# A two-layer decoder trunk on one core: low parts in pieces of 256 columns on GpSimd, and the delta net's convolution shared differently between VectorE and ScalarE

## The chip, the cores and the metric

The kernel runs on one core of a Trainium2 chip. A core has TensorE (PE in the profile; PEld is its loading of weights), VectorE (DVE), ScalarE (ACT), GpSimd (POOL) and SyncE (SP, which issues DMAs here). The engines run at the same time, each through its own list of instructions in order, and wait for each other by semaphores. Data lie in SBUF (128 partitions) and products land in PSUM (banks of 128 x 512 f32). The metric is the device time of one execution in microseconds (us).

## The reference

Two layers over 1024 tokens of width 1024. Layer 0 mixes tokens by RWKV-7, layer 1 by a gated DeltaNet; each is followed by a dense SwiGLU part, with layer norms and a modulation from a conditioning vector. The change touches two things: the split of f32 operands into a high and a low part, which the kernel uses for every dense product, and the delta net's projections with their causal convolution of four taps:

```python
def _gated_deltanet_mixer(u, w_in, conv_w, a_log, dt_bias, norm_g, w_out):
    ...
    proj = u @ w_in
    qkv = jax.nn.silu(_causal_depthwise_conv(proj[..., :3 * hd], conv_w))
    z = proj[..., 3 * hd:4 * hd].reshape(B, T, H, d)
    ...
    q = _l2norm(qkv[..., :hd].reshape(B, T, H, d)) * d ** -0.5
    k = _l2norm(qkv[..., hd:2 * hd].reshape(B, T, H, d))
    v = qkv[..., 2 * hd:].reshape(B, T, H, d)
    ...
    o = _chunk_gated_delta_rule(q, k, v, g, beta)
    o = _rms_norm(o, norm_g, 1e-6) * jax.nn.silu(z.astype(F32))
    return o.reshape(B, T, hd).astype(u.dtype) @ w_out
```

## The kernel before

The tokens are handled in two halves of 512 columns; channels lie on partitions, eight groups of 128. Every dense product is made of three: weight high times activation high, weight high times activation low, weight low times activation high (`mm3`, L258 to L263). A high part is a copy in a reduced f32 form, a low part the difference of the source and its high part (`split`, L220 to L225; the difference is recorded as L212, the line of the helper `tt`). One weight is 128 x 1024 (all eight groups of input channels for 128 outputs), so one output tile takes 24 matmuls of 512 columns.

`weight` (L238) brings one weight: a DMA into `wr` (2 buffers), the high part `wh` by ACT, the low part `wl` by POOL unless the caller names DVE (3 buffers each). A low part that is needed again for the second half of the tokens is stored to memory by SP (L236) and read back there instead of being computed a second time. So POOL makes low parts mostly while the first half of a layer's weights passes: for the RWKV projections, the first dense half of layer 0 (about 700 to 1400 us, woven with the RWKV units), the delta net's projections for the first half of the tokens (1500 to 1720 us) and the first dense half of layer 1 (2460 to 2820 us, woven with the delta net's heads).

`proj_gdn(h, kinds)` (L1264) makes the delta net's projections of half `h`, tile by tile. `kinds` (1, 0) are k and q, eight tiles each, in the function `turn` (L1486); `kinds` (4,) are v and z in turns, woven with the heads and the dense part. A tile of k, q or v goes this way: eight times three matmuls into a PSUM bank `mm`; ACT copies the bank to `x` (L1289, columns 3 to 514); DVE puts zeros ahead of it and saves the last three columns in `ctail` for the second half (L1292, L1293), or takes them from `ctail` (L1295); DVE makes the last tap (L1296, a multiplication by a number per partition) and adds the other three (L1298, recorded as L215); ACT takes tanh (L1303), DVE makes silu from it (L1304, recorded as L215), SP stores the tile. For k and q ACT squares it into `th` (L1307), and the next call of `flush` hands the squares to PE, which sums them over the partitions into the bank `rows` (`sums`, L338). `flush` stood behind the next tile's matmuls. After the eighth tile of a kind `rows_out` turns the sums into factors on DVE.

The pieces are Python generators. `interleave` (L971) and `weave` (L775) draw from several of them by costs written at each `yield`; so the code of a projection tile is issued among that of layer norms, gates or heads. The framework then sets each engine's list from this, may move an instruction ahead of or behind others where its operands allow it (the sums of squares stand in the middle of a later tile's matmuls), and adds the waits. Tiles come from pools with a fixed number of buffers for each name: `e` has 5 (here `x`, the tile and `th` of each projection), `rows` 2 banks and `mm` 6 banks in `turn`.

## Time and profile before

| | |
|---|---|
| median of 3 runs | 3426.49 us (3426.42 to 3430.7) |
| the profiled execution | 3418.32 us |
| its span, first to last instruction | 3416.5 us |
| TensorE's mean granted clock | 0.970 |
| PE, PEld busy | 3229.8, 2464.8 us |
| DVE, ACT, POOL busy | 2207.9, 1374.5, 974.0 us |

The span is read by stages, since the engines that PE waits for differ between them. Idle time of an engine that nobody waits for costs nothing; what counts here are PE's waits, and in front of them the DVE operation or the ACT operation that ended late. A duration in the timeline runs from the start of an instruction to its end and holds whatever the instruction waits for once it has been issued.

### The profile page before, as it was taken

What the parts mean: (1) busy time and instruction counts of PE and PEld (TensorE: products, weight loads), DVE (VectorE), ACT (ScalarE), POOL (GpSimd) and SP (SyncE); (2) the same over time, 40 slices, a digit from 0 to 9 for tenths busy, and PEclk for the clock granted to TensorE, in tenths of its full rate; (3) what the DMA queues carried; (4) which work ended last, traced back from release to release, by engine and by line L of the source; (5) the groups of instructions that cost most, each with busy time, mean ns of one, the idle gap of its engine ahead of it and who ended that gap; (6) DMA issues with size and microseconds to landing.
All of it is one profiled execution on the core that took longest, in us unless ns stands there. A gap on an engine that the chain in (4) does not pass through costs nothing. (4 is left out here: it accounts for less than half of the span.)

```text
span 3416.5 us, 51830 instructions
## 1 busy us (share of the span) xinstructions
PE 3229.8 (95%) x19408; PEld 2464.8 (72%) x19408; DVE 2207.9 (65%) x4630; ACT 1374.5 (40%) x2622; POOL 974.0 (29%) x725
## 2 busy tenths in 40 slices
PE   7989999988999999988999999999989999999997
PEld 3667777765666676766777777777767778878886
DVE  5667888877666666587676555586577763573235
ACT  4656777634333333344332222345323223342222
POOL 2443233343333333443321000220133333420001
PEclk8999999997999999999999999999999999999998
DMA  7872334352444444644664554556644446565543
GB/s 260 274 242 89 114 106 132 122 171 82 159 148 165 145 165 141 217 165 175 223 209 166 182 170 168 199 187 218 223 166 157 151 151 235 182 209 185 197 174 135
DMA packets 240524, 594.12 MB, mean 174 GB/s; under 512 B 24720, under 2 KB 80656, under 8 KB 240272
## 3 DMA queue, kind: packets, MB, share of 16 engines
q1 hardware_dynamic: 240128, 590.74, 51.1%
q8 instruction: 152, 2.49, 0.3%
q14 instruction: 100, 0.82, 0.1%
q10 hardware_dynamic: 144, 0.07, 0.0%
HBM read 440.04 MB, written 150.67 MB: 173 GB/s over the span
## 5 line engine op out<-in xcount | busy, mean ns | idle before, releaser
L261 PE MATMUL mm<-s,wh 128*128 128x512 f32 x2608 | 1081.3, 415 | 14.0 <-DVE s L224 5.9
L262 PE MATMUL mm<-s,wh 128*128 128x512 f32 x2608 | 1057.9, 406 | 14.6 <-DVE s L212 8.2
L263 PE MATMUL mm<-s,wl 128*128 128x512 f32 x2608 | 1050.0, 403 | 0.0
L212 POOL TENSOR_TENSOR wl<-wr,wh 128x1024 fp32r<-128x1024 f32 (+1 forms) x243 | 504.4, 2082 | 981.9 <-ACT wh L222 912.4
L261 PEld LDWEIGHTS mm<-s,wh 128*128 128x128 f32 x2608 | 497.4, 191 | 129.2 <-issue 19.8
L262 PEld LDWEIGHTS mm<-s,wh 128*128 128x128 f32 x2608 | 498.4, 191 | 112.3 <-DVE s L212 12.7
L263 PEld LDWEIGHTS mm<-s,wl 128*128 128x128 f32 x2608 | 497.5, 191 | 95.1 <-issue 1.2
L249 ACT CAST wh<-wr 128x1024 fp32r<-128x1024 f32 x199 | 206.6, 1049 | 500.4 <-PE mm L262 260.3
L222 ACT CAST wh<-wr 128x1024 fp32r<-128x1024 f32 (+1 forms) x254 | 228.2, 905 | 343.9 <-PE mm L262 201.1
L215 DVE SCALAR_TENSOR_TENSOR x<-mm,modp,x 128x512 f32<-128x512 f32 x272 | 202.1, 747 | 73.9 <-PE mm L263 72.0
L261 PE MATMUL mm<-ys,wh 128*128 128x512 f32 x544 | 219.6, 404 | 2.9 <-DVE x L215 2.8
L262 PE MATMUL mm<-ys,wh 128*128 128x512 f32 x544 | 217.3, 400 | 0.0
L263 PE MATMUL mm<-ys,wl 128*128 128x512 f32 x544 | 217.3, 399 | 0.0
L212 DVE TENSOR_TENSOR e<-mm,e 128x512 f32<-128x512 f32 x88 | 60.6, 689 | 168.7 <-PE mm L263 168.4
L212 DVE TENSOR_TENSOR s<-e,s 128x512 fp32r<-128x512 f32 x106 | 122.2, 1154 | 60.8 <-ACT s L222 60.6
L833 PEld LDWEIGHTS <-z 128*128 128x128 f16 x1600 | 83.8, 98 | 103.3 <-issue 64.2
L215 DVE SCALAR_TENSOR_TENSOR e<-e,mm 128x512 f32<-128x512 f32 x88 | 60.2, 684 | 141.8 <-ACT e L676 141.4
L215 DVE SCALAR_TENSOR_TENSOR tx<-mm,modp,tx 128x512 f32<-128x512 f32 x112 | 83.1, 748 | 79.4 <-PE mm L263 79.1
L261 PEld LDWEIGHTS mm<-ys,wh 128*128 128x128 f32 x544 | 103.7, 191 | 29.7 <-DVE x L215 3.7
L263 PEld LDWEIGHTS mm<-ys,wl 128*128 128x128 f32 x544 | 103.5, 190 | 25.7
L262 PEld LDWEIGHTS mm<-ys,wh 128*128 128x128 f32 x544 | 103.7, 191 | 25.2 <-issue 0.5
L215 DVE SCALAR_TENSOR_TENSOR e<-e,vec,e 128x512 f32<-128x512 f32 x144 | 115.0, 799 | 3.8
(389 smaller groups left out, 5418.8 us busy)
## 6 DMA issues: line engine op xcount, KB each, us to landing
wr<-w_in SPq DMA_DIRECT2D x176, 512.0 KB, 4.5
ada<-ada_w SPq DMA_DIRECT2D x96, 512.0 KB, 4.8
loi<-wl SPq DMA_DIRECT2D x88, 512.0 KB, 3.0
wr<-w_ffo SPq DMA_DIRECT2D x88, 512.0 KB, 4.9
wl<-loi SPq DMA_DIRECT2D x88, 512.0 KB, 3.6
wr<-w_g SPq DMA_DIRECT2D x64, 512.0 KB, 4.5
lof<-wl SPq DMA_DIRECT2D x44, 512.0 KB, 2.9
wl<-lof SPq DMA_DIRECT2D x44, 512.0 KB, 3.5
```

Source lines behind the costliest of these rows:

```text
L212: eng.tensor_tensor(out=out, in0=a, in1=b, op=op)
L215: return dve.scalar_tensor_tensor(out=out, in0=a, scalar=s, in1=b, op0=op0, op1=op1)
L222: act.copy(out=hi, in_=src)
L249: act.copy(out=hi[:, :], in_=raw[:, :])
L261: pe.matmul(out, wh[:, off:off + P], ah, start=start, stop=False)
L262: pe.matmul(out, wh[:, off:off + P], al, start=False, stop=False)
L263: pe.matmul(out, wl[:, off:off + P], ah, start=False, stop=stop)
L833: pe.matmul(out, l, r, start=start, stop=stop)
```

## The change

Three things change.

1. `split`: a low part that is not made by DVE is made in pieces of at most 256 columns, each an instruction of its own. A weight's low part on POOL becomes four instructions, one of an activation (512 columns) two. Parts of 128 or 256 columns stay as they are, and so do DVE's.
2. The convolution: in the first half ACT saves the last three columns, straight from PSUM; in the second ACT puts them ahead of `x`. The last tap is made by ACT from PSUM (Copy with a scale per partition) and not by DVE from `x`. This is for k, q and v, 24 tiles in each half.
3. The sums of squares: `flush(1)` keeps one tile back, so a tile's sums are handed to PE behind the matmuls of the second tile after it. `th` of k and q has a pool of its own with 4 buffers and no longer uses `e`.

```diff
--- before.py
+++ after.py
@@ -222,7 +222,10 @@
             act.copy(out=hi, in_=src)
         else:
             hi_eng.tensor_copy(out=hi, in_=src)
-        tt(lo_eng or pool, lo, src, hi.bitcast(F32), SUB)
+        eng, n = lo_eng or pool, src.shape[-1]
+        step = n if eng is dve else min(n, 256)
+        for o in range(0, n, step):
+            tt(eng, lo[:, o:o + step], src[:, o:o + step], hi[:, o:o + step].bitcast(F32), SUB)
 
     flip = [0]
 
@@ -1261,17 +1264,18 @@
         act.activation(out=gt["ekd"][:, :, :], in_=x, func=AF.Exp)
         yield 1.0
 
-    def proj_gdn(h, kinds):
+    def proj_gdn(h, kinds, tp=None):
+
         u = uu[h]
         rows = {}
         late = []
 
-        def flush():
-            for kind, j, th in late:
+        def flush(keep=0):
+            while len(late) > keep:
+                kind, j, th = late.pop(0)
                 sums(rows[kind], C("gsel"), j, th)
                 if j == 7:
                     rows_out(qk_d[h][kind], rows[kind], 4e-6, 128.0 ** -0.5 if kind == 0 else None)
-            late.clear()
 
         for grp in kinds:
             if grp in (0, 1):
@@ -1284,22 +1288,22 @@
                     mm3(pst[:, :], w, P * k, u[k], k == 0, k == KT - 1)
                     if GY and k < KT - 1:
                         yield 0.65
-                flush()
+                flush(1)
                 x, o = e3_tile(), e_tile()
                 act.copy(out=x[:, 3:], in_=pst[:, :])
                 if kind < 3:
                     if h == 0:
                         dve.memset(x[:, 0:3], 0.0)
-                        dve.tensor_copy(out=pools["ctail"][:, m, :], in_=x[:, HT:HT + 3])
+                        act.copy(out=pools["ctail"][:, m, :], in_=pst[:, HT - 3:HT])
                     else:
-                        dve.tensor_copy(out=x[:, 0:3], in_=pools["ctail"][:, m, :])
-                    dve.tensor_scalar(out=o[:, :], in0=x[:, 3:], scalar1=V("conv", 4 * m + 3), scalar2=None, op0=MUL)
+                        act.copy(out=x[:, 0:3], in_=pools["ctail"][:, m, :])
+                    act.activation(out=o[:, :], in_=pst[:, :], func=AF.Copy, scale=V("conv", 4 * m + 3))
                     for tap in range(3):
                         stt(o[:, :], x[:, tap:tap + HT], V("conv", 4 * m + tap), o[:, :], MUL, ADD)
                     src = o[:, :]
                 else:
                     src = x[:, 3:]
-                th = e_tile()
+                th = tl(tp, [P, HT], F32, "th", 4)[:, :] if kind < 2 else e_tile()
                 act.activation(out=th[:, :], in_=src, func=AF.Tanh, scale=0.5)
                 stt(o[:, :], th[:, :], 1.0, src, ADD, MUL)
                 sync.dma_start(out=g_d[h][m][:, :], in_=o[:, :])
@@ -1489,7 +1493,7 @@
             with tc.tile_pool(name=f"tp{l}{h}", bufs=1, reuse_waits="tile") as tp:
                 side = seq(norm1(l, h), gdn_gates(h))
                 drive(interleave([out_proj(out_l, out_h, tp), itertools.islice(side, TI)], [1.0, TC[0]]))
-                drive(interleave([proj_gdn(h, (1, 0)), side, norm0(out_l, out_h, True)], [1.0, TC[1], TC[2]]))
+                drive(interleave([proj_gdn(h, (1, 0), tp), side, norm0(out_l, out_h, True)], [1.0, TC[1], TC[2]]))
 
         turn(0, 0, 0, 1)
         with tc.tile_pool(name="gp0", bufs=1, reuse_waits="tile") as gp:
```

In the list of PE, first half of the tokens, the sums (32x128 x4, into `rows`) of the first k tile, before: `mm_4334` is the bank of the third k tile, `e_4317` holds the squares of the first.

```order
L262 MATMUL mm_4334_18193<-s_4263_17840,wh_4331_18187 128x512
L263 MATMUL mm_4334_18193<-s_4262_17839,wl_4332_18188 128x512
L261 MATMUL mm_4334_18193<-s_4265_17846,wh_4331_18187 128x512
L338 MATMUL rows_4309_18030<-e_4317_18073,cst_1_66 32x128 x4
L262 MATMUL mm_4334_18193<-s_4266_17847,wh_4331_18187 128x512
L263 MATMUL mm_4334_18193<-s_4265_17846,wl_4332_18188 128x512
```

The same sums after the change (`th_4317` holds the squares, `mm_4342` is the bank of the fourth tile; line numbers are 3 higher):

```order
L265 MATMUL mm_4334_18505<-s_4281_18210,wh_4331_18496 128x512
L266 MATMUL mm_4334_18505<-s_4280_18209,wl_4332_18497 128x512
L341 MATMUL rows_4309_18337<-th_4317_18383,cst_1_66 32x128 x4
L264 MATMUL mm_4342_18559<-s_4247_18080,wh_4339_18550 128x512
L265 MATMUL mm_4342_18559<-s_4248_18081,wh_4339_18550 128x512
L266 MATMUL mm_4342_18559<-s_4247_18080,wl_4340_18551 128x512
```

They stood behind 13 of the third tile's 24 matmuls and stand behind all 24 now. Over the sixteen tiles of the first half the place moves by 6 to 18 matmuls, except for the last two, which the end of the projection sets.

In the list of DVE, q tiles of the first half, before (`e_4435` is `x` of a tile, `e_4436` the tile, `e_4437` its `th`):

```order
L1292 MEMSET e_4435_18725 128x3
L215 SCALAR_TENSOR_TENSOR e_4428_18675<-e_4429_18683,e_4428_18675 128x512
L1293 COPY ctail_4184_17488<-e_4435_18725 128x3
L1296 TENSOR_SCALAR e_4436_18726<-e_4435_18725,vec_2_67 128x512
L215 SCALAR_TENSOR_TENSOR e_4436_18726<-e_4435_18725,vec_2_67,e_4436_18726 128x512 x3
L1292 MEMSET e_4443_18776 128x3
L215 SCALAR_TENSOR_TENSOR e_4436_18726<-e_4437_18734,e_4436_18726 128x512
```

And after (`e_4443` and `e_4451` are `x` of two tiles, `th` has its own name):

```order
L1296 MEMSET e_4451_19172 128x3
L215 SCALAR_TENSOR_TENSOR e_4444_19119<-e_4443_19118,vec_2_67,e_4444_19119 128x512 x3
L215 SCALAR_TENSOR_TENSOR e_4444_19119<-th_4445_19127,e_4444_19119 128x512
L1296 MEMSET e_4459_19226 128x3
L215 SCALAR_TENSOR_TENSOR e_4452_19173<-e_4451_19172,vec_2_67,e_4452_19173 128x512 x3
L215 SCALAR_TENSOR_TENSOR e_4452_19173<-th_4453_19181,e_4452_19173 128x512
```

A tile had seven instructions on DVE and has five: the copy to `ctail` and the multiplication are gone.

In the list of ACT at the same place, before (`e_4443` is `x` of a tile, `e_4444` the tile, `wh_4471` the high part of a weight that comes later):

```order
L1307 ACTIVATE e_4437_18734<-e_4436_18726 128x512
L1289 COPY e_4443_18776<-mm_4442_18747 128x512
L1303 ACTIVATE e_4445_18785<-e_4444_18777 128x512
L222 CAST wh_4471_18945<-wr_4470_18943 128x1024
L1307 ACTIVATE e_4445_18785<-e_4444_18777 128x512
L1289 COPY e_4451_18827<-mm_4450_18798 128x512
```

And after:

```order
L1293 COPY e_4443_19118<-mm_4442_19089 128x512
L1297 COPY ctail_4184_17786<-mm_4442_19089 128x3
L1300 ACTIVATE e_4444_19119<-mm_4442_19089,vec_2_67 128x512
L1307 ACTIVATE th_4445_19127<-e_4444_19119 128x512
L222 CAST wh_4471_19296<-wr_4470_19294 128x1024
L1311 ACTIVATE th_4445_19127<-e_4444_19119 128x512
```

The two operations stand between the copy out of PSUM and the tanh, which still waits for DVE's three taps. On POOL the rows `wl` of 128x1024 became `128x256 x4` at the same places. PE waits for the pieces one by one: in a tile's 24 matmuls the waits for POOL stand at the first, third, fifth and seventh matmul with the low part, where before one stood at the first.

## Rows read from the trace of the kernel before

**Rows 1.** The page: from part 1 the line of PE and the engines beside it (busy time, share of the span, instructions), from part 5 the group of the products with the weights' low parts (busy time, mean ns of one, then the idle time of PE just before them), and from part 6 the DMAs that bring a delta-net weight (count, size, median us to landing).

```profile
PE 3229.8 (95%) x19408; PEld 2464.8 (72%) x19408; DVE 2207.9 (65%) x4630; ACT 1374.5 (40%) x2622; POOL 974.0 (29%) x725
...
L263 PE MATMUL mm<-s,wl 128*128 128x512 f32 x2608 | 1050.0, 403 | 0.0
...
wr<-w_g SPq DMA_DIRECT2D x64, 512.0 KB, 4.5
```

**Rows 2.** The table of windows, by stage: the stretch in us, its length, then busy us (and instructions) of PE, PEld, DVE, ACT and POOL, the granted clock, DMA share and GB/s. 700:1400 is the RWKV units beside the first dense half, 1514:1642 and 1642:1720 the projections of the delta net for the first half of the tokens (the second stretch runs into the heads), 2204:2460 the turn for the second half, 2460:2820 the heads beside the dense half after it.

```profile
700.00:1400.00 700.00, 651.15 (x4305) 469.63 (x4305) 482.14 (x1186) 243.65 (x507) 271.81 (x209) 0.94 0.45 149
...
1514.00:1642.00 128.00, 110.91 (x577) 84.06 (x577) 101.25 (x170) 54.99 (x86) 42.86 (x18) 0.96 0.49 173
1642.00:1720.00 78.00, 78.00 (x345) 64.56 (x344) 52.37 (x66) 30.75 (x44) 30.72 (x13) 1.00 0.72 248
...
2204.00:2460.00 256.00, 247.45 (x1188) 193.82 (x1189) 165.26 (x283) 118.34 (x173) 34.50 (x20) 0.97 0.62 207
2460.00:2820.00 360.00, 332.48 (x2092) 259.38 (x2091) 263.62 (x565) 106.27 (x208) 140.11 (x77) 0.98 0.47 158
```

**Rows 3.** The list of who PE waited for, 1514 to 1642 us: us in total, times, longest.

```profile
PE rows L338 <- ACT e L1307: 17.0, 11, 3.7
```

**Rows 4.** The same list, 2260 to 2460 us (second half of the tokens).

```profile
PE rows L338 <- ACT e L1307: 1.4, 1, 1.4
```

**Rows 5.** The timeline of one tile's end, 1574 to 1581 us: start, duration, engine, line, operation and tiles, and in brackets the idle time before with what ended it.

```profile
1575.42 2.39 POOL L212 TENSOR_TENSOR wl<-wr,wh 128x1024 fp32r<-128x1024 f32 x1 [5.29 <-ACT wh L222]
...
1575.91 2.46 DVE L215 SCALAR_TENSOR_TENSOR e<-e,e 128x512 f32<-128x512 f32 x1 [2.39 <-ACT e L1303]
...
1578.39 0.63 ACT L1307 ACTIVATE e<-e 128x512 f32<-128x512 f32 x1 [2.52 <-DVE e L215]
...
1579.08 0.43 PE L338 MATMUL rows<-e,cst 128*32 128x128 f32 x8 [1.68 <-ACT e L1307]
```

**Rows 6.** The timeline at 1260 us, in the dense half beside the RWKV units, same columns.

```profile
1260.68 2.36 POOL L212 TENSOR_TENSOR wl<-wr,wh 128x1024 fp32r<-128x1024 f32 x1 [5.39 <-ACT wh L222]
...
1261.16 2.44 DVE L212 TENSOR_TENSOR s<-e,s 128x512 fp32r<-128x512 f32 x1 [1.48 <-ACT s L222]
...
1263.95 0.29 DVE L212 TENSOR_TENSOR ix<-pa,stack 128x128 f16<-128x128 f32 x1
...
1264.30 0.25 PE L833 MATMUL pa<-ix,z 128*128 128x32 f16 x4 [2.75 <-DVE ix L212]
```

**Rows 7.** The timeline at 2533 us, where two weights' low parts stand one behind the other on POOL (x2), same columns.

```profile
2533.04 4.71 POOL L212 TENSOR_TENSOR wl<-wr,wh 128x1024 fp32r<-128x1024 f32 x2 [14.11 <-ACT wh L222]
...
2533.17 2.30 DVE L215 SCALAR_TENSOR_TENSOR gt<-gt,gv 128x4 f32<-128x4 f32 x1
...
2535.39 0.74 DVE L215 SCALAR_TENSOR_TENSOR x<-mm,modp,x 128x512 f32<-128x512 f32 x1
...
2536.05 1.72 DVE L215 SCALAR_TENSOR_TENSOR gt<-gt 128x4 f32<-128x4 f32 x1
```

**Rows 8.** Groups of POOL's subtractions over the whole run, different shapes apart: count, busy us, mean ns of one, idle before.

```profile
L212 POOL TENSOR_TENSOR wl<-wr,wh 128x1024 fp32r<-128x1024 f32 x195 | 471.7, 2423 | 900.7 <-ACT wh L222 852.9 <-PE mm L263 7.6 <-PE pc L1395 7.4
...
L212 POOL TENSOR_TENSOR s<-e,s 128x512 fp32r<-128x512 f32 x24 | 35.8, 1502 | 64.7 <-ACT s L222 42.3 <-DVE s L224 18.1 <-DVE gm L215 2.6
...
L212 POOL TENSOR_TENSOR yo<-yo,bv 128x256 f32<-128x256 f32 x32 | 26.4, 824 | 114.4 <-ACT yo L1180 102.1 <-DMA ada<-ada_w 6.8 <-PE pc L1124 5.5
...
L212 POOL TENSOR_TENSOR g2l<-g2r,g2h 128x128 fp32r<-128x128 f32 x16 | 8.2, 514 | 7.8 <-ACT g2h L222 7.8
```

**Rows 9.** Groups of DVE, 1440 to 1720 us, the convolution's among them: count, busy us, mean ns of one, idle before.

```profile
L215 DVE SCALAR_TENSOR_TENSOR e<-e,vec,e 128x512 f32<-128x512 f32 x72 | 61.0, 848 | 1.9
L215 DVE SCALAR_TENSOR_TENSOR e<-e,e 128x512 f32<-128x512 f32 x30 | 38.1, 1269 | 27.5 <-ACT e L1303 27.5
L1293 DVE COPY ctail<-e 128x3 f32<-128x3 f32 x24 | 24.9, 1037 | 17.6 <-ACT e L1289 17.6
L1296 DVE TENSOR_SCALAR e<-e,vec 128x512 f32<-128x512 f32 x24 | 11.4, 476 | 0.0
```

**Rows 10.** From part 5 of the page: DVE's low parts of activations, and a DVE operation of the same size with one input from PSUM.

```profile
L212 DVE TENSOR_TENSOR e<-mm,e 128x512 f32<-128x512 f32 x88 | 60.6, 689 | 168.7 <-PE mm L263 168.4
L212 DVE TENSOR_TENSOR s<-e,s 128x512 fp32r<-128x512 f32 x106 | 122.2, 1154 | 60.8 <-ACT s L222 60.6
```

**Rows 11.** Groups of ACT over the whole run, shapes apart: a weight's high part, and an operation that reads a bank of PSUM with a scale per partition.

```profile
L222 ACT CAST wh<-wr 128x1024 fp32r<-128x1024 f32 x206 | 214.3, 1047 | 338.6 <-PE mm L262 201.1 <-issue 63.0 <-DMA wr<-w_in 22.0
...
L475 ACT ACTIVATE e<-mm,vec 128x512 f32<-128x512 f32 x16 | 11.1, 692 | 0.0
```

**Rows 12.** Groups of ACT, 1440 to 1720 us: the smallest operation that reads PSUM there with all 128 partitions.

```profile
L1257 ACT ACTIVATE g_gl<-mm 128x32 f32<-128x32 f32 x1 | 0.2, 198 | 0.5 <-DVE g_gc L1256 0.5
```

**Rows 13.** The table of windows in steps of 10 us, columns as in rows 2.

```profile
1560.00:1570.00 10.00, 6.29 (x27) 4.59 (x26) 8.49 (x11) 3.88 (x6) 5.29 (x3) 0.83 0.67 237
...
1580.00:1590.00 10.00, 9.07 (x39) 6.84 (x38) 8.91 (x20) 2.68 (x4) 2.39 (x1) 0.83 0.39 134
...
1620.00:1630.00 10.00, 7.00 (x38) 5.08 (x39) 6.81 (x10) 3.65 (x7) 4.74 (x2) 0.89 0.45 158
```

**Rows 14.** The list of who PE waited for, 700 to 1400 us.

```profile
PE pc L1133 <- DVE w L212: 12.6, 8, 3.7
PE pa L833 <- DVE ixt L212: 9.8, 5, 3.1
```

## The prediction

> **What bounds the kernel now.** I read part 1 of the page first: PE is busy for 3229.8 of 3416.5 us [rows 1], so no more than 187 us can be won without taking work from PE, and the question is which of PE's waits the change touches. The table of windows by stage comes next [rows 2]. In 1642:1720 PE is busy for all of 78.00 us with 345 matmuls, 0.226 us each at a granted clock of 1.00: that is the pace at which nothing else matters, and a projection tile of 24 matmuls takes 5.44 us at it. The idle time lies elsewhere: 17.1 us in 1514:1642, 48.9 in 700:1400, 27.5 in 2460:2820, 8.6 in 2204:2460. The list of waits says what it is. In 1514:1642 it has one line, PE waiting for ACT's squares before the sums, 17.0 us in 11 waits [rows 3]; in the second half of the tokens the same line has 1.4 us [rows 4].
>
> The timeline shows why the two halves differ [rows 5]. POOL begins a low part at 1575.42 and takes 2.39 us. DVE's silu, begun at 1575.91, takes 2.46 us and ends 0.56 us behind POOL, where a DVE operation of this size with one input from PSUM has a mean of 0.69 us [rows 10]. ACT's square waits 2.52 us for it, PE 1.68 us for the square. So a DVE operation with both inputs in SBUF stands still while a POOL instruction runs. In the groups: the silu has a mean of 1269 ns, and the copy of three columns to `ctail` 1037 ns [rows 9]; DVE's low parts of activations have 1154 ns against 689 for the neighbour with a PSUM input [rows 10]. In the second half POOL makes no low parts of these weights. The Trainium skill (SBUF — State Buffer, section "SBUF: two separate sides") says that DVE and GpSimd share a port pair which one instruction holds to its end while the other is blocked; the trace agrees, 2.46 us for 0.69.
>
> In 700:1400 the waits are spread over the RWKV units' chains [rows 14], and behind many of them stands the same thing: at 1260 us a low part of an activation is held for 2.44 us by a weight's low part of 2.36 us, the small operations queued behind it come late, and PE waits 2.75 us for one of them [rows 6].
>
> **The change part by part, costed against the profiled execution (3418.3 us).**
>
> *Sums one tile later.* The order moves the sums of a first-half tile by 6 to 18 matmuls, 1.4 to 4.1 us at 0.226. The eleven waits have a mean of 1.55 and a longest of 3.7 us [rows 3]. Besides, the squares come earlier: DVE's copy and multiplication, 1037 + 476 ns [rows 9], become two ACT operations, for which the nearest rows are 198 ns (128x32 from PSUM) [rows 12] and 692 ns (128x512 from PSUM with a scale) [rows 11], so 0.6 us less per tile; and the silu can be held by a piece only. I take 15 of the 17.0 us, and 1 of 1.4 in the second half; bounds 10 and 18.4. What is late next is nothing at the start of such a tile: its weights' products never wait (the low-part products have 0.0 us of idle time in the whole run [rows 1]).
>
> *The clock after these waits.* Of the 10-us windows around them three have a granted clock of 0.83, 0.83 and 0.89 [rows 13]: PE ran at 1.2 GHz for part of each, after being idle. That is 4.5 us of pace lost; part of it falls into idle time, so I take 3.
>
> *ACT's new work.* 48 tiles by 0.692 + 0.198 us is 43 us on an engine that is busy for 55 of 128 us in the densest stretch [rows 2]. It hides beside PE's 5.44 us per tile: two PSUM readings more per tile against six `mm` banks. I cost it at nothing; if ACT's order puts it ahead of a weight's high part, it is 0.9 us against a lead of two tiles. In the v and z tiles beside the heads DVE loses 0.48 us per tile, also off PE's path: nothing.
>
> *Pieces on POOL.* A subtraction has means of 514 ns for 128 columns, 824 for 256, 2423 for 1024 [rows 8]: four pieces take about 3.30 us, 0.87 more than one whole, 170 us of POOL time over 195 weights. Alone this reaches nobody, as PE has no idle time at the low parts, and PE takes the first piece 1.6 us earlier than it took the whole. PE's list gets three more waits for POOL per tile, with the rest of the tile queued behind each; waits that are met cost nothing in 1642:1720, where the pace of 0.226 us holds with them [rows 2], and the last piece is needed some 4 us after the first. Other POOL work behind a weight comes later by 0.9 us; I charge 2 us. The Trainium skill (GPSIMD Engine Reference, section 3.1) gives about 2.6 cycles per element and 4497 ns for 2048 columns, which leaves some 60 ns of fixed cost in one instruction. By it, an estimate, the pieces cost 0.2 us more per weight and not 0.87; the rows show the larger price here.
>
> What the pieces give: a DVE operation that meets a low part now waits for at most 0.82 us and not 2.42, about a third. But the next one is stopped by the next piece. This order of turns is in the trace: with two low parts back to back [rows 7] a small DVE operation waits through the first (2.30 us), an operation with a PSUM input runs beside the second at its free 0.74 us, and the next small one waits through the second (1.72 us). So one operation in a stretch of POOL work gains two thirds of its wait; four in a row gain nothing and lose 0.9 us. Idle time of PE in the two woven stretches is 48.9 + 27.5 = 76.4 us. I take three quarters of it as standing behind a held operation (a reading of rows 6 and of many like it, so the softest number here), and of the two thirds that a single operation gains, half, because of the chains: 76.4 x 0.75 x 0.33 = 19 us. Bounds: nothing (all chains) and 38 us (all single).
>
> *Sum.* 15 + 1 + 3 + 19 - 2 = 36 us: 3418.3 - 36 = 3382.3 us for an execution like the profiled one. The profiled one lies 8.2 us under the median of the runs, 3426.5; the forecast for the median is 3426.5 - 36, rounded to **3391 us**.
>
> **Rivals.**
>
> A, *the pieces give nothing*: DVE's operations mostly come in rows of four and more, so each piece stops one. For it: a convolution tile has three taps in a row and a layer norm's inverse root seven small operations. Against: in the weave they stand between operations with PSUM inputs, which run beside POOL [rows 7]. Then 15 + 1 + 3 - 2 = 17 us remain: 3409 us.
>
> B, *the pieces free nearly everything*: 38 us, and the clock with it. 700:1400 has a granted clock of 0.94 [rows 2], 42 us of pace; a third of that is 14. 15 + 1 + 3 + 38 + 14 = 71 us: 3355 us. Against: the RWKV chains are long, and PE's next wait in them is often behind the first.
>
> C, *the weights come late* (the slower side). A raw weight has two buffers, so landing 4.5 us [rows 1], high part 1.05 [rows 11] and low part must fit in two tiles, 10.9 us. Before: 4.5 + 1.05 + 2.4 = 8.0. After, with a DVE operation let in at 0.56 us between pieces [rows 5]: 3.3 + 3 x 0.56 = 5.0, loop 10.5. From a low part of 5.3 us on it decides: one more microsecond of landing gives 11.5, 0.3 us lost per weight, and over the half of 195 weights at PE's full pace 29 us, with the 19 us of the pieces gone: 3426.5 - 17 + 29 = 3438 us. Against it: idle time 0.0 at the low parts [rows 1], and PE takes the pieces one by one.
>
> D, *the wait for the sums only moves*: DVE is busy for 101 of 128 us in 1514:1642 [rows 2] with a layer norm between the tiles; were it the bound there, later sums would wait again for two thirds, and with no gain from the pieces 5 us remain: 3421 us. Against: 24 tiles lose 1.5 us each on DVE, 36 us in 1514:1720.
>
> **How the numbers follow.** Forecast 0.60, A 0.18, B 0.08, C 0.07, D 0.07. A measurement of this kernel tells 0.2% (7 us) from no change. The forecast's own range is 3369 (pieces 38 us, sums 18) to 3415 (pieces near nothing, sums 10); to hold 8 in 10 I reach down toward B and up to D: 3364 to 3424. Faster: the forecast, A and B nearly whole, 0.83; same: D and edges of A, 0.11; slower: C less its edge, 0.06.
>
> **What would show it.** In the profile after: PE's line for the sums in the first half near 0 to 2 us and clocks of 1.00 in those windows; DVE's silu and low parts of activations nearer 0.8 us than 1.2; `wl` pieces of 0.75 to 0.9 us; the `ctail` copies on ACT near 0.2; idle time of 700:1400 near 36 us. The forecast is wrong if idle time at the low-part products appears (C), if the sums still wait 10 us (D), or if DVE's mean of a held group stays above 1.1 us (A).

## The result and the profile after

The changed kernel takes 3378.2 us (median of 4 executions, 3375.8 to 3386.2) against 3426.5 for the kernel before (4 executions, 3422.1 to 3430.7): ratio 0.987, 95% interval 0.985 to 0.989. That is 44 us by the ratio (48 between the two medians), and more than the 36 forecast. The profiled execution of it lasted 3386.16 us (span 3384.4), the slowest of the four, so the two profiles are only 32 us apart.

The page, in the lines that answer to [rows 1]:

```profile
PE 3222.6 (95%) x19408; PEld 2462.3 (73%) x19408; DVE 2074.1 (61%) x4534; ACT 1405.1 (42%) x2718; POOL 1129.7 (33%) x1353
...
L266 PE MATMUL mm<-s,wl 128*128 128x512 f32 x2608 | 1047.8, 402 | 0.0
...
wr<-w_g SPq DMA_DIRECT2D x64, 512.0 KB, 4.6
```

PE's idle time fell from 186.7 to 161.8 us, DVE's busy time by 134 us, POOL's rose by 156. Nothing waits at the low-part products. By stage, as in [rows 2] (all later stages begin earlier now: 1503:1618 lies within what was 1514:1642, with 540 of its 577 matmuls, and 2431:2790 answers to 2460:2820; the stretch with the very same matmuls as 1514:1642 is given as the last row):

```profile
700.00:1400.00 700.00, 662.21 (x4418) 480.45 (x4417) 463.89 (x1202) 250.65 (x516) 319.14 (x415) 0.96 0.47 156
1503.00:1618.00 115.00, 106.30 (x540) 80.66 (x539) 81.55 (x133) 63.68 (x115) 59.11 (x68) 0.94 0.53 185
1618.00:1696.00 78.00, 78.00 (x345) 64.56 (x344) 36.43 (x51) 35.17 (x57) 44.02 (x50) 1.00 0.73 250
...
2431.00:2790.00 359.00, 338.45 (x2117) 264.80 (x2116) 239.96 (x564) 108.73 (x212) 170.92 (x202) 0.98 0.48 163
```

```profile
1500.58:1619.16 118.58, 109.88 (x577) 83.65 (x577) 84.54 (x136) 65.55 (x121) 61.34 (x70) 0.94 0.55 189
```

Idle time is length less PE's busy time: 37.8 us for 48.9 in 700:1400, 20.6 for 27.5 in 2431:2790, 8.7 for 17.1 in the last row. In 1618:1696 three more waits for POOL per tile cost nothing: the same 345 matmuls in the same 78.00 us.

The place of [rows 6] shows the mechanism undisturbed. The timeline of the same instructions now:

```profile
1250.95 2.55 POOL L212 TENSOR_TENSOR wl<-wr,wh 128x256 fp32r<-128x256 f32 x3 [4.78 <-ACT wh L222]
...
1251.43 0.81 DVE L212 TENSOR_TENSOR s<-e,s 128x512 fp32r<-128x512 f32 x1 [1.66 <-ACT s L222]
...
1252.59 0.29 DVE L212 TENSOR_TENSOR ix<-pa,stack 128x128 f16<-128x128 f32 x1
...
1252.93 0.25 PE L836 MATMUL pa<-ix,z 128*128 128x32 f16 x4 [1.30 <-DVE ix L212]
```

DVE's subtraction is let in behind the first piece: 0.81 us where it took 2.44. The small operation behind it and PE's product come earlier, and PE waits 1.30 us and not 2.75. The groups over the whole run say the same of all such places (compare [rows 8, 10], 2423 and 1154 ns):

```profile
L212 POOL TENSOR_TENSOR wl<-wr,wh 128x256 fp32r<-128x256 f32 x780 | 623.4, 831 | 799.0 <-ACT wh L222 761.5 <-DMA lor<-wl 8.7 <-PE mm L266 7.6
```

```profile
L212 DVE TENSOR_TENSOR s<-e,s 128x512 fp32r<-128x512 f32 x106 | 84.1, 795 | 70.6 <-ACT s L222 70.3
```

The sums' wait is less well answered. The list of who PE waited for, 1503 to 1618 us [rows 3]:

```profile
PE rows L341 <- ACT th L1311: 8.6, 5, 5.8
```

Half of 17.0 is left, in fewer and longer waits. The timeline of a q tile shows a part of why; it repeats tile by tile up to the longest wait, the 5.8 us in its last line:

```profile
1590.76 0.56 ACT L1293 COPY e<-mm 128x512 f32<-128x512 f32 x1
...
1591.22 0.16 ACT L1297 COPY ctail<-mm 128x3 f32<-128x3 f32 x1
...
1591.27 0.70 ACT L1300 ACTIVATE e<-mm,vec 128x512 f32<-128x512 f32 x1
...
1592.01 2.99 DVE L215 SCALAR_TENSOR_TENSOR e<-e,vec,e 128x512 f32<-128x512 f32 x3 [1.89 <-ACT e L1300]
...
1595.03 0.63 ACT L1307 ACTIVATE th<-e 128x512 f32<-128x512 f32 x1 [3.05 <-DVE e L215]
...
1595.57 1.04 ACT L222 CAST wh<-wr 128x1024 fp32r<-128x1024 f32 x1
...
1595.69 0.69 DVE L215 SCALAR_TENSOR_TENSOR e<-th,e 128x512 f32<-128x512 f32 x1 [0.70 <-ACT th L1307]
...
1596.51 0.62 ACT L1311 ACTIVATE th<-e 128x512 f32<-128x512 f32 x1
...
1597.04 0.56 ACT L1293 COPY e<-mm 128x512 f32<-128x512 f32 x1
...
1597.18 0.42 PE L341 MATMUL rows<-th,cst 128*32 128x128 f32 x8 [0.19 <-ACT th L1311]
...
1603.42 0.66 PE L341 MATMUL rows<-th,cst 128*32 128x128 f32 x8 [5.81 <-ACT th L1311]
```

From one copy out of PSUM to the next it is a closed chain of ACT and DVE: copy, last tap, three taps on DVE, tanh, then a weight's high part beside DVE's silu, square, next copy. It takes 6.28 us. PE's own step is a tile with the sums behind it, and where PE waits for nothing it takes 6.02 us:

```profile
1566.20 0.43 PE L341 MATMUL rows<-th,cst 128*32 128x128 f32 x8
...
1572.23 0.43 PE L341 MATMUL rows<-th,cst 128*32 128x128 f32 x8
```

So the chain falls behind PE by 0.26 us per tile, and the waits at the sums of these tiles are as small: 0.27, 0.15 and 0.19 us. Most of the lead was gone before them. These are ACT's copies of the 9th to the 13th tile, and the first operation on DVE of the factors of k (`rows_out`), which it makes between the taps until 1569.5 us:

```profile
1554.89 0.56 ACT L1293 COPY e<-mm 128x512 f32<-128x512 f32 x1
...
1563.28 0.57 ACT L1293 COPY e<-mm 128x512 f32<-128x512 f32 x1
...
1570.71 0.57 ACT L1293 COPY e<-mm 128x512 f32<-128x512 f32 x1
...
1578.00 0.58 ACT L1293 COPY e<-mm 128x512 f32<-128x512 f32 x1
...
1584.48 0.56 ACT L1293 COPY e<-mm 128x512 f32<-128x512 f32 x1
```

```profile
1562.63 0.28 DVE L348 TENSOR_SCALAR e<-rows 128x128 f32<-128x128 f32 x1
```

Over these four tiles the copy falls from 0.7 to 6.2 us behind the end of its tile's matmuls; how much of that is the factors' doing no run separates. The longest wait then shows the lag at one place. At the end of the projection the sums of the 15th tile stand directly behind those of the 14th, with no tile's matmuls between them, so PE waits there for a whole turn of the chain: 5.8 of the 8.6 us. In the kernel before 17 matmuls stood between these two, and PE waited 2.3 us:

```profile
1627.50 0.42 PE L338 MATMUL rows<-e,cst 128*32 128x128 f32 x8 [2.29 <-ACT e L1307]
```

### The profile page after: what moved, and what is told of

The parts are those of the page before. It is cut to its first block, busy times and chain, and to the rows that moved or that the text cites. A ratio compares the mean times of both kernels' runs of the same rounds, so it can differ in the third digit from the quotient of the medians.

```text
span 3384.4 us, 52492 instructions
## 1 busy us (share of the span) xinstructions
PE 3222.6 (95%) x19408; PEld 2462.3 (73%) x19408; DVE 2074.1 (61%) x4534; ACT 1405.1 (42%) x2718; POOL 1129.7 (33%) x1353
## 4 chain that ended last, share of the span: by engine, by line
PE 43%; DVE 4%; ACT 2%; DMA 2%; issue 2%; POOL 2%; SPq 0%; ACTq 0%; POOLq 0%; DVEq 0%
PE mm L264 13%; PE mm L265 12%; PE mm L266 12%; PE pa L836 1%; DVE e L215 1%; POOL wl L212 1%; PE p L1354 1%; DMA wr<-w_in 1%; ACT wh L222 1%; PE pc L1388 0%; PE pc L1392 0%; DMA yr<-y 0%; PE p L1336 0%; PE pc L1397 0%; PE pc L1399 0%
## 5 line engine op out<-in xcount | busy, mean ns | idle before, releaser
L212 POOL TENSOR_TENSOR wl<-wr,wh 128x256 fp32r<-128x256 f32 (+1 forms) x828 | 651.3, 817 | 876.7 <-ACT wh L222 829.4
L215 DVE SCALAR_TENSOR_TENSOR e<-e,vec,e 128x512 f32<-128x512 f32 x144 | 124.2, 866 | 97.2 <-ACT e L1300 89.9
L212 DVE TENSOR_TENSOR s<-e,s 128x512 fp32r<-128x512 f32 x106 | 84.1, 795 | 70.6 <-ACT s L222 70.3
```

Of the source, the lines that this page charges most:

```text
L212: eng.tensor_tensor(out=out, in0=a, in1=b, op=op)
L215: return dve.scalar_tensor_tensor(out=out, in0=a, scalar=s, in1=b, op0=op0, op1=op1)
```

## The experiments

A time below is the median of a kernel's executions, a ratio with its 95% interval is against the kernel before on the same chip (median 3421 to 3424 us in these runs), and gains are by the ratio. Two executions of one kernel differ by up to 30 us, so an interval is some 5 to 8 us wide on each side. For stages I set the borders of [rows 2] at the same matmul in each trace.

**One part at a time.** The theory of the first result: a POOL instruction stops DVE until it ends, pieces cut that stop, and this carries most of the gain. The rival: the convolution and the later sums carry it.

*Pieces alone* (the kernel before with this edit):

```diff
-        tt(lo_eng or pool, lo, src, hi.bitcast(F32), SUB)
+        eng, n = lo_eng or pool, src.shape[-1]
+        step = n if eng is dve else min(n, 256)
+        for o in range(0, n, step):
+            tt(eng, lo[:, o:o + step], src[:, o:o + step], hi[:, o:o + step].bitcast(F32), SUB)
```

> The kernel before with the pieces on GpSimd alone. Theory M (a GpSimd instruction holds VectorE's operation until it ends, so pieces cut each hold to a third): 20 to 28 us faster than before; idle time of PE in 700:1400 falls by about 11 us and in the heads beside the second dense half by about 7; VectorE's low parts of activations have a mean near 0.8 us and not 1.15; PE's wait for the squares in the projections falls from 17 to about 12 us. Rival R1 (the gain of the whole change is the convolution's and the sums'): within 7 us of before. Rival R2 (PE gains because it gets the first piece of a weight earlier): faster, but VectorE's means stay at 1.15 us and the idle time that goes is ahead of the low-part products.

3384.4 us, ratio 0.9886 (0.9865 to 0.9908): 39 us, most of what the whole change gives and more than expected. The stage that holds the sums has another picture:

```profile
PE rows L341 <- ACT e L1310: 13.0, 11, 2.3
```

Still eleven waits, only shorter. DVE's groups there (1417 to 1691 us) show what [rows 9] showed with 848, 1269, 1037 and 476 ns:

```profile
L215 DVE SCALAR_TENSOR_TENSOR e<-e,vec,e 128x512 f32<-128x512 f32 x72 | 64.3, 893 | 1.9
L215 DVE SCALAR_TENSOR_TENSOR e<-e,e 128x512 f32<-128x512 f32 x32 | 25.0, 782 | 26.4 <-ACT e L1306 26.4
L1299 DVE TENSOR_SCALAR e<-e,vec 128x512 f32<-128x512 f32 x24 | 20.3, 848 | 0.0
L1296 DVE COPY ctail<-e 128x3 f32<-128x3 f32 x24 | 9.6, 400 | 25.3 <-ACT e L1292 25.3
```

The copy and the silu gain 0.64 and 0.49 us, and the operations in the row behind them lose about half of it again: the last tap goes from 0.48 to 0.85, each of the three others from 0.85 to 0.89. These are means over k, q and v; the chain of a q tile (6.84 us before, 6.80 now) gains next to nothing from pieces. That is rival A, true here and not in the weave.

*All but the pieces*:

```diff
-        eng, n = lo_eng or pool, src.shape[-1]
-        step = n if eng is dve else min(n, 256)
-        for o in range(0, n, step):
-            tt(eng, lo[:, o:o + step], src[:, o:o + step], hi[:, o:o + step].bitcast(F32), SUB)
+        tt(lo_eng or pool, lo, src, hi.bitcast(F32), SUB)
```

> The whole change without the pieces. Theory M: 12 to 22 us faster than before, so 25 to 35 us slower than the changed kernel; in 700:1400 PE's idle time is that of before, 49 us. Rival R1: 40 to 48 us faster than before, as the changed kernel. If the parts need each other (rival R3: with whole low parts the loop of ScalarE and VectorE eats the lead of the later sums at once): under 8 us faster.

3415.8 us, 0.9983 (0.9969 to 0.9997): 6 us, less than the theory had. Under 8 us is what R3 had expected, but its reason, that the parts need each other, isn't borne out: the parts add up (39 + 6 = 45, against 44 for the whole).

*Later sums alone* (the kernel before with the edits of `flush`, its call, and the buffers of `th`):

```diff
-                flush()
+                flush(1)
...
-                th = e_tile()
+                th = tl(tp, [P, HT], F32, "th", 4)[:, :] if kind < 2 else e_tile()
```

> The kernel before with the later sums (and the separate buffers of the squares) alone. My prediction's term: 11 to 16 us faster, the wait for the squares 17.0 to 2 us. Theory L (a tile goes through ScalarE and VectorE in a closed loop that is longer than PE's 5.44 us, since the square of a tile stands ahead of the next tile's copy out of PSUM on ScalarE; the lead of one more tile is eaten within a few tiles): 3 to 9 us faster, with few but long waits for the squares, 8 to 14 us in all and the longest over 4 us. Rival R3: within 3 us.

3414.9 us, 0.9984 (0.9969 to 0.9999): 5.5 us. The list of waits in that stage:

```profile
PE rows L338 <- ACT th L1308: 15.6, 7, 6.4
```

The lead of one more tile turns eleven waits into seven, and 17.0 us into 15.6. My term of 15 us falls. The waits are few and long, as L had it, but more than its 8 to 14 us, and 6.4 of the 15.6 is the one wait at the end of the projection, 2.3 us before. The chain, 6.85 us per tile here, costs 0.5 to 0.8 us at each of three sums ahead of it.

*The convolution alone* (the kernel before with the edits on L1293 to L1296):

```diff
-                        dve.tensor_copy(out=pools["ctail"][:, m, :], in_=x[:, HT:HT + 3])
+                        act.copy(out=pools["ctail"][:, m, :], in_=pst[:, HT - 3:HT])
...
-                    dve.tensor_scalar(out=o[:, :], in0=x[:, 3:], scalar1=V("conv", 4 * m + 3), scalar2=None, op0=MUL)
+                    act.activation(out=o[:, :], in_=pst[:, :], func=AF.Copy, scale=V("conv", 4 * m + 3))
```

> The kernel before with the last tap and the saved columns on ScalarE alone. Theory L: VectorE's copy that was held for 1.04 us and its multiplication of 0.48 us leave the loop and ScalarE's 0.16 + 0.69 us enter it, so the loop is 0.6 us shorter per tile and the wait for the squares falls from 17 to 8 to 12 us: 5 to 10 us faster. Rival R4 (ScalarE's two more operations per tile come at the price of the high parts of weights and cost what VectorE gains): within 3 us. Rival R1: 15 us or more faster.

3420.8 us, 0.9998 (0.9984 to 1.0013): no difference in the total that can be told. L had expected 5 to 10 us; within 3 is what R4 had. In the stage the chain is shorter as expected (6.20 us per tile) and so is the wait for the squares, but PE now also waits once for a weight's low part, which it didn't before:

```profile
PE rows L338 <- ACT e L1307: 10.9, 5, 3.4
PE mm L263 <- POOL wl L212: 1.4, 1, 1.4
```

So R4's price is there in small (1.5 us with whole low parts and both other edits, nothing in the changed kernel); it leaves 3.4 us of gain in this stage, and where the total loses them again isn't shown.

**What about the pieces counts: length, number, or the first one's arrival?** All three are edits of the changed kernel.

```diff
-        step = n if eng is dve else min(n, 256)
+        step = n if eng is dve else min(n, 128)
```

> The changed kernel with pieces of 128 columns (eight instructions per weight). Theory M, with the hold as long as one piece: a piece of 128 columns took 0.51 to 0.60 us, so the hold falls from 0.83 to 0.6 us and gives up to 5 us more; but eight pieces take 4.1 to 4.8 us by themselves and over 5.44 us, a tile of PE, with turns given to VectorE, so in the projections low-part products would wait (theory C of my prediction). I expect 0 to 15 us slower than the changed kernel, with idle time ahead of the low-part products. Rival (a piece's fixed part can be neglected): 3 to 6 us faster than the changed kernel, no idle time there.

```diff
-        step = n if eng is dve else min(n, 256)
+        step = n if eng is dve else min(n, 512)
```

> The changed kernel with pieces of 512 columns (two instructions per weight, an activation's part whole). Theory M: the hold is 1.3 to 1.4 us, between 0.83 and 2.42; by these lengths about a third of the pieces' gain of 38 us is lost: 10 to 16 us slower than the changed kernel, 30 to 38 us faster than before; VectorE's low parts have a mean near 0.95 us. Rival (what matters is that a weight's low part is cut at all, so that a waiting operation gets its turn): within 5 us of the changed kernel. Rival (only short holds are harmless): 25 us or more slower than the changed kernel.

```diff
-        for o in range(0, n, step):
+        for o in reversed(range(0, n, step)):
```

> The changed kernel with the four pieces of a low part made in reverse, so that TensorE's first product with a low part needs the piece made last, about 0.9 us later than the whole low part came before the change. Theory M (VectorE's holds are what counts): as the changed kernel within 5 us. Rival R2 (TensorE gains because the first piece comes 1.6 us earlier): most of the gain goes, 25 to 38 us slower than the changed kernel, with idle time ahead of the low-part products.

Pieces of 128: 3397.3 us, 0.9928 (0.9913 to 0.9942). Of 512: 3385.3, 0.9895 (0.9877 to 0.9913). In reverse: 3380.7, 0.9884 (0.9866 to 0.9902). The last settles the rival of the early first piece: the order is turned round, low-part products idle for 3.9 us in the whole run, and the gain stays. For the length, the same stage of the other two:

```profile
700.00:1400.00 700.00, 656.78 (x4346) 474.31 (x4344) 472.14 (x1193) 246.45 (x509) 291.35 (x274) 0.95 0.47 154
```

```profile
700.00:1400.00 700.00, 663.53 (x4419) 479.11 (x4418) 457.24 (x1207) 250.92 (x518) 367.70 (x698) 0.96 0.48 156
```

One low-part instruction has a mean of 2.42, 1.40, 0.83 and 0.53 us (1024, 512, 256, 128 columns); PE's idle time in the stage is 48.9, 43.2, 37.8 and 36.5 us. A straight line through the first and third (7.0 us of idle per us of instruction) gives 41.8 and 35.7 for the other two. So PE's idle time here follows the length of the instruction. (Kernels with the same pieces differ in it by 1.2 us at 256 columns and by 2.4 at 1024, so the step from 256 to 128 is at the edge of what one profile tells.) In the total, 512 columns are 9 us behind 256 by the ratios, just under the 10 to 16 I had expected, and their intervals overlap. The Trainium skill (SBUF — State Buffer, "SBUF: two separate sides") describes this as a lock that an instruction holds to its end; these four lengths agree.

Pieces of 128 lose 20 us by the ratios, more than the 15 I had allowed, and not at the weights as I had expected (those products still have 0.0 us of idle time). From the list of waits of the whole run, changed kernel and then pieces of 128:

```profile
PE mm L265 <- POOL s L212: 7.6, 8, 3.0
...
PE mm L264 <- ACT s L222: 5.4, 3, 3.5
```

```profile
PE mm L265 <- POOL s L212: 16.6, 11, 4.4
PE mm L264 <- ACT s L222: 10.3, 3, 6.0
```

These are low and high parts of activations, which PE does wait for, and which now come later. That is 14 us of the 20; the rest I didn't place.

**What limits the projections?** The theory now: the chain of one tile through ACT and DVE. First only the square is put behind the next copy:

```diff
                 if kind < 2:
-                    act.activation(out=th[:, :], in_=o[:, :], func=AF.Square)
+                    sq.append((th, o))
                     late.append((kind, j, th))
...
                     act.activation(out=o[:, :], in_=pst[:, :], func=AF.Copy, scale=V("conv", 4 * m + 3))
+                    square()
```

> The changed kernel with the square of a tile put behind the next tile's copies out of PSUM on ScalarE. In the q tiles the loop from one copy to the next then loses the silu and the square: 6.25 us become about 5.0, below TensorE's 5.44 and the sums' 0.25. Theory L (this loop eats the lead of the sums): the wait for the squares in the first half falls from 8.6 to under 3 us and 1503:1618 gains 5 to 9 us; in the total 3 to 9 us faster than the changed kernel. Rival (VectorE's holds set the last wait, in whatever order ScalarE works): the wait stays at 7 to 10 us and the time within 3 us of the changed kernel.

3383.1 us, 0.9897 (0.9875 to 0.9918): no gain on the changed kernel. PE's list in the stage (1484 to 1601 us):

```profile
PE mm L264 <- ACT e L1306: 4.8, 1, 4.8
PE rows L341 <- ACT th L1277: 3.9, 4, 1.8
```

The wait for the squares has halved, as expected, but the idle time is 8.7 us as before it: the rest is now a wait for a bank of PSUM that ACT's last tap gives back. I had left the high part of a weight out of the chain: ACT makes it (1.03 us) between tanh and the next copy, and the taps take 3.16 us, so the chain is 5.93 us and not 5.0. That is about PE's own 6.02: the lag, 6.1 us at the 12th tile and 5.9 at the 14th, no longer grows, but it isn't made up either. Which wait comes last only shows where it surfaces.

Then two tiles in flight, with tanh pinned behind the next tile's last tap:

```diff
-                th = tl(tp, [P, HT], F32, "th", 4)[:, :] if kind < 2 else e_tile()
-                act.activation(out=th[:, :], in_=src, func=AF.Tanh, scale=0.5)
...
+                finish(end if kind < 2 else None)
+                rest.append((kind, j, m, src, o))
...
+        def finish(after=None):
+            while rest:
+                kind, j, m, src, o = rest.pop(0)
...
+                with tc.issue_after(after.ins) if after else ExitStack():
+                    act.activation(out=th[:, :], in_=src, func=AF.Tanh, scale=0.5)
```

> The changed kernel with tanh, silu, store and square of a k or q tile emitted behind the next tile's copies and taps, and the tanh held in its place behind the next tile's last tap on ScalarE (two tiles in flight). Theory T (in the projections of the first half the pace is set by what a tile takes through ScalarE and VectorE one after the other: 6.84 us before, 6.28 after, 5.93 with the square later, against 5.69 for TensorE; whichever wait of TensorE comes last only shows the lag): the spacing of the copies in the q tiles falls to 5.7 us or below, TensorE's idle time in this stage from 8.7 to under 3 us, and the stage gains 5 to 10 us: 3372 to 3380 us in all. Rival (the order within ScalarE's list isn't the limit, VectorE's busy time with its holds is): spacing stays over 5.9 us and idle time over 7 us.

```profile
PE rows L341 <- ACT th L1283: 5.4, 3, 3.1
```

The idle time of the stage falls from 8.7 to 5.4 us and the stage is 5.1 us shorter, at the lower edge of what was expected, and the idle time isn't down to under 3 us. That it is the opened chain isn't shown: with this edit a tile's squares are also handed on one tile later, so its sums stand behind the matmuls of the third tile after it, a further tile of lead, and at the last tile ACT's copy is still 5.6 us behind PE (6.3 in the changed kernel). A kernel with that lead alone was not run. ACT's timeline shows what is late next:

```profile
1575.31 1.05 ACT L222 CAST wh<-wr 128x1024 fp32r<-128x1024 f32 x1 [3.21 <-DMA wr<-w_g]
1576.27 0.58 ACT L1306 COPY e<-mm 128x512 f32<-128x512 f32 x1
...
1594.44 1.05 ACT L222 CAST wh<-wr 128x1024 fp32r<-128x1024 f32 x1 [3.79 <-DMA wr<-w_g]
1595.40 0.58 ACT L1306 COPY e<-mm 128x512 f32<-128x512 f32 x1
```

Copies come 4.1 to 8.7 us apart at the end and no longer evenly, and where a high part of a weight stands ahead of a copy, ACT now waits for that weight's DMA. The stage in eight of the kernels, at the same matmuls:

| kernel | copies of the last q tiles, us apart | stage 1514:1642, us | PE idle in it, us |
|---|---|---|---|
| before | 6.84 | 127.9 | 17.1 |
| later sums alone | 6.85 | 126.6 | 15.6 |
| convolution alone | 6.20 | 124.5 | 13.5 |
| both | 6.18 | 124.4 | 14.3 |
| pieces alone | 6.80 | 120.9 | 13.2 |
| the whole change | 6.28 | 118.6 | 8.7 |
| square later too | 5.93 | 116.9 | 8.7 |
| two tiles in flight | 4.1 to 8.7 | 113.4 | 5.4 |

Among the kernels with the same code in this stage (the changed one, reverse, weights only, all pieces) it takes 116.6 to 118.9 us with 8.4 to 9.3 of idle time, so two microseconds tell nothing; two tiles in flight were run twice (113.4 and, with weights only, 113.3 us). Pieces alone shorten the stage by 7.0 us at an almost unchanged spacing (6.80), so the spacing of the last tiles alone doesn't set its length.

The total of two tiles in flight, 3380.2 us (0.9881, 0.9863 to 0.99), doesn't show these 5 us: the interval is wider.

**Can more be had from pieces?** Weights alone in pieces, then this with two tiles in flight, then all of POOL's operations of 512 columns in two:

```diff
-        step = n if eng is dve else min(n, 256)
+        step = n if eng is dve or n < 1024 else 256
```

> The changed kernel with pieces for weights alone: GpSimd makes the low parts of activations (512 columns) whole again. Cost suspected of these pieces: TensorE's waits for GpSimd's and VectorE's low parts of activations are 13.8 us in all before, 11.3 after, 17.9 with pieces of 128 columns. Theory M: the weights' pieces carry the gain, so within 5 us of the changed kernel, with 1 to 4 us less wait for GpSimd's low parts of activations. Rival (activations' pieces count too): 5 us or more slower.

> Both of the last two edits on the changed kernel, as a version meant to beat it. Theory T and M: the sum of both, 5 to 12 us faster than the changed kernel, 3366 to 3376 us. Rival: within 4 us of the changed kernel.

```diff
     def tt(eng, out, a, b, op):
+        if eng is pool:
+            if len(out.shape) == 2 and out.shape[-1] == 512:
+                for o in (0, 256):
+                    pool.tensor_tensor(out=out[:, o:o + 256], in0=a[:, o:o + 256], in1=b[:, o:o + 256], op=op)
+                return
...
```

> The changed kernel with GpSimd's other operations of 512 columns (some 130 subtractions, products and sums of layer norms, RWKV units and delta-net heads, 1.3 to 1.6 us each) cut in two as well. Theory M by length of the hold: they hold VectorE for 1.35 us at most, 0.8 after; by their busy time of about 180 us against 472 and the shorter cut this is worth 3 to 5 us. Against it, the results come 0.2 to 0.4 us later, and VectorE and TensorE wait for some of them. I expect within 5 us of the changed kernel, idle time in 700:1400 by 0 to 2 us lower than 37.8. Rival (cutting costs where another engine waits for the whole result, as with the activations' low parts): 5 to 12 us slower, idle time of 700:1400 above 39.

3386.0 (0.9896, 0.9881 to 0.9911), 3383.4 (0.9886, 0.9869 to 0.9902) and 3380.9 us (0.9874, 0.9851 to 0.9897). The intervals of all three overlap that of the changed kernel (0.985 to 0.989); no version here is shown to beat it. Weights alone are 9 us behind it by the ratios, nearer to the rival than to the 5 us expected: PE's waits for POOL's low parts of activations fell by 2.6 us as expected, but those for DVE's rose by 3.0. The 5 to 12 us expected of both edits together did not come. The last is within 5 us of the changed kernel, as expected; its idle time, 155.7 us in its profile against 161.8, is lower by a little, with 37.5 us in 700:1400.

## Why the prediction was right, and where it was not

The time lies 13 us under the forecast and inside the range, faster as expected. But the sum was right by two errors of opposite sign, and that is luck.

- **Sums one tile later, 15 + 1 us, and the clock after these waits, 3: mis-sized, the step that failed.** Sums and convolution together gave 6 us by the runs. I costed the move as a delay that covers each wait, and said that nothing is late next. Two things stood against it. The last two tiles, which the end of the projection sets, are in the order lists and got no price: the sums of the 15th tile lost the matmuls ahead of them, and PE's wait there grew from 2.3 to 5.8 us (6.4 with later sums alone). And a delay covers a wait that comes once; it does not cover a lag that stays. ACT's copies are 6 us behind PE from the 12th tile on, and for those tiles the chain's 6.28 us against PE's 6.02 leaves no room to catch up. The spacing of ACT's copies stood in the trace of before: 6.84 us. I set PE's pace at 5.44 from [rows 2], which is the tile without its sums; the expectations' 0.25 for these is too little, the step with them is 6.02. Of my rivals D came nearest (later sums wait again). Its reason, DVE with other work between the tiles, is in the trace at the 10th and 11th tile (the factors of k); in the last tiles it is the chain, and no run parts the two. The convolution's 0.6 us per tile was right (6.84 to 6.20).
- **The clock of these windows didn't come back**: 0.94 in 1503:1618, for 0.96 in [rows 2]. Behind the one wait of 5.8 us PE's matmuls start 0.43 us apart and not 0.226 until 1609.3 us: a granted clock of 0.5, 1.2 GHz. With pieces alone, where the longest of eleven waits is 2.3 us, the same matmuls have 0.99:

```profile
1488.07:1608.97 120.90, 107.67 (x578) 81.80 (x577) 94.87 (x170) 55.00 (x86) 58.26 (x70) 0.99 0.54 186
```

- **Pieces, 19 - 2 us: mis-sized the other way.** They gave 39. For the idle time of the two woven stages the step held: 48.9 + 27.5 us fell by 11.1 + 7.0 = 18 against 19, though no run shows either of its two factors (three quarters, and half of two thirds) by itself. What I left out is what else moves with it. Means over the profiled executions of four kernels with whole low parts and eight with pieces of 256: stage 700:1400 is 21.8 us shorter, of which 12.0 are idle time and 9.8 pace. By the granted clock in windows of 10 us, PE ran at 1.2 and not 2.4 GHz for 79 us of this stage before, for 54 in the kernel with pieces alone. This varies from one execution to the next (70 to 87 us in the four, 37 to 75 in the eight), so the pace's part is less sure than the idle time's. I gave that term to rival B alone (14 us) and nothing of it to the forecast. (B's sum also leaves out the 2 us that the other sums charge; it would be 69 us.) The heads beside the second dense half are 7.0 us shorter by the same means, and the two turns gave the rest: 7.0 us for pieces alone in the first (3.9 idle), 4.5 in the second as a mean.
- **The extra POOL time cost nothing with 256 columns**, as argued: the DMA lands in 4.6 us, low-part products never wait. Rival C's way (weights late) didn't happen even with 128 columns; what is late then are activations' parts.
- **ACT's new work at nothing** held as far as can be told: convolution alone gives no loss in the total, with one wait of 1.4 us for a weight's low part. `ctail` on ACT takes 0.16 us, the last tap 0.70, as bounded. It does stand in the chain, though.
- **Rival A's rule is right by place**: a row of taps gains nothing from pieces, a single operation between PSUM readers gains two thirds.

What stays open: why executions of one kernel differ by up to 30 us. The idle time of 700:1400 is 37 to 38 us in all eight kernels with pieces of 256, its length 671 to 686 us; the difference is the granted clock, and what sets that from one execution to the next no run here tells.

## What to carry to other kernels

An instruction on POOL with both inputs in SBUF stopped DVE operations on SBUF here for as long as it ran itself (2.44 us beside 2.36), while those with an input from PSUM ran beside it (0.74 us, [rows 7]). Where single DVE operations stand on the path, cut it, to the length at which its results are still early; don't cut what TensorE waits for. Before moving a consumer one tile later, measure the spacing of the producer's tiles and set it against the consumer's whole step, here 6.02 us and not 5.44. A lead helps against a late tile, and not against a chain that is longer than that step. Price the place where the row of tiles ends, too: there consumers can come to stand one behind the other, and the whole lag shows in one wait (5.8 of 8.6 us here). Idle time that goes can give back clock as well: in 700:1400 nearly as much again, in the projections of the changed kernel nothing.

## What the runs showed of the hardware

- Turn-taking is strict enough to move time between neighbours: with pieces the 3-column copy on DVE fell from 1037 to 400 ns, and the multiplication right behind it rose from 476 to 848 ns.
- A low part costs POOL more the finer it is cut: 2.42 us whole, 2.8 in two, 3.3 in four, 4.2 in eight (mean of one times count, with what DVE takes between), and none of that reached PE at the weights.
